# Output projection of a hybrid decoder layer by Strassen's seven products, with shared code and accumulating DMAs for the weight sums

## The chip, the core and the metric

The kernel runs on one NeuronCore of one Trainium2 chip. Five engines work from their own instruction queues and meet at semaphores: TensorE (PE: matmuls and transposes, results in PSUM banks of 128 x 512 float32), VectorE (DVE: elementwise work), ScalarE (ACT: activations, casts), GpSimd (POOL: here only reciprocal roots, and the issue of accumulating DMAs), SyncE (SP: the issue of plain DMAs). The metric is the device time of one execution in microseconds.

## The reference

One layer over 512 tokens and 1024 channels, in float32:

```python
u = _rmsnorm(h, norm1_g[l]);  proj = u @ w_in[l]           # GLU | q k v | r | decay | gates A, B
y_conv = silu(layernorm(dwconv31(glu))) @ w_conv_out[l]
y_gla  = (headwise_rmsnorm(gla(q, k, v, decay)) * silu(r)) @ w_gla_out[l]
merged = sigmoid(gate_a) * y_conv + sigmoid(gate_b) * y_gla
h = h + merged @ w_o[l]                                    # the output projection, 1024 x 1024
u2 = _rmsnorm(h, norm2_g[l])
z = dwconv3(u2 @ w_ffn_up[l])                              # 2 x 2816 channels
h = h + (silu(z[..., :F]) * z[..., F:]) @ w_ffn_down[l]    # the down projection, 2816 x 1024
return _rmsnorm(h, final_g)
```

## The kernel before

Every matrix product is done as three matmuls in the float32r type: each operand is split into a high part (an ACT cast, `whi` for weights) and a low part (a DVE subtraction, `wlo`), and `mm3` (L281 to 287) adds low x high, high x low and high x high into one PSUM bank. Activations lie with channels on partitions, 8 tiles of 128 channels by 512 tokens.

The weights form one long list, `order`. `load` issues the DMA of the next entry on SP into a `raw` tile (three buffers), `split_weight` splits it into `whi`/`wlo` (four buffers each), and `weight` hands the next entry to the products after it has split two entries ahead (`LOOK`). All queues run in order; in the loops spoken of here the framework's planner sets the order of the instructions on each engine from the data they share.

The stages around the change are: `w_gla` and `w_ga` products; eight `w_conv` column tiles of 24 matmuls (`col_tile`), each followed on DVE by a gate product, a sum and a split (`split`); the output projection; then the up projection with its 3-tap convolution and gate, in three `GROUPS` of channel pairs, each followed by a down projection.

The output projection before goes by `row_half`: for each half `n` of the output columns, four token tiles, eight channel tiles, three matmuls. In the second half the token tiles come one after another; `o_done` (L794) loads the residual `x`, adds it to the bank, squares it on ACT, and for `n == 1` forms the root on POOL (`rsqrt`, L333) and the normed tile `un` on DVE. `to_channels` (L355) transposes `un` on PE, four transposes to a bank, casts it on ACT (`uh`) and subtracts on DVE (`ul`). Tiles 0 and 1 are transposed inside the products of tiles 2 and 3, tile 2 at the end, and tile 3 after the second column tile of the up projection, whose first four column tiles (`w_up`, 256 tokens at a time) use tokens 0 to 255 first.

The down projection before (`down`, L902) already goes by Strassen's seven products in Winograd's form: the 512 tokens are two halves, the channels of a group two halves (the first and second of each pair), the output columns two halves. `STEPS` names the products `a11`, `a12`, `s1`, `n2`, `s4`, `n3`, `a22`, each with one or two weight blocks (`d`). `first_of_pair` and `second_of_pair` form the sums of activations. The weight sums are made in three ways: by accumulating DMAs on POOL (`kept` after `a11`, L226; `raw` of `n3`, L193), by a DVE addition at `n2` (L200) and by a DVE addition at `a22` (L200).

Of the kernel before, what the change touches and what calls it, by code (L numbers as in the profile page):

```python
# [10 lines left out]
F32 = mybir.dt.float32  # L11
# [20 lines left out]
EPS = 1e-6  # L32
GROUPS = (((0, 2), (1, 3), (4, 6), (5, 7)), ((8, 10), (9, 11), (20, 21)), ((12, 14), (13, 15), (16, 18), (17, 19)))
# [5 lines left out]
ET = mybir.EngineType  # L39

# [22 lines left out]
def trunk_layer(ctx: ExitStack, tc: tile.TileContext, a: dict, out: bass.AP):  # L63
# [84 lines left out]
    for m in range(KT):  # L148
        order += [("w_conv", m)]
    order += [("w_o", j) for j in range(KT)]  # L150
    for gi, pairs in enumerate(GROUPS):
        order += [("w_up", j) for pair in pairs for i in pair for j in (i, FT + i)]
        order += [("w_down", (gi, step, d)) for step, d in STEPS]
# [5 lines left out]
    def load():  # L159
        if len(raws) < len(order):  # L160
            name, j = order[len(raws)]
            if name == "w_down":
                raws.append(load_down(*j))
                return
            raw = wp.tile([P, D], F32, tag="raw", name=nm("raw"), bufs=3)
            nc.sync.dma_start(raw, a[name][j])
            raws.append(raw)


    def down_block(gi, d, row, col):  # L170

        pairs = GROUPS[gi][2 * d : 2 * d + 2]
        first = pairs[0][row]
        j = col * (FT // 2) + first // 2
        if len(pairs) == 2:
            return a["w_down"][j]
        return a["w_down"][j][:, row * T : (row + 1) * T]

    def load_down(gi, step, d):

        if step in ("s1", "s4"):
            return None
        row, col = {"a11": (0, 0), "a12": (1, 0), "n2": (1, 1), "n3": (0, 1), "a22": (1, 0)}[step]
        src = down_block(gi, d, row, col)
        if step in ("a11", "n2"):
            raw = fp.tile([P, D], F32, tag="kept", name=nm("kept"), bufs=4)
            kept[gi, d, "t" if step == "a11" else "b22"] = raw
        else:
            raw = wp.tile([P, D], F32, tag="raw", name=nm("raw"), bufs=3)
        n = src.shape[-1]  # L190
        nc.sync.dma_start(raw[:, :n], src)
        if step == "n3":
            nc.gpsimd.dma_start(raw[:, :n], down_block(gi, d, 1, 1), accum_op=ALU.add)  # L193
        return raw[:, :n]

    def sum_down(raw, gi, step, d):

        n = T * len(GROUPS[gi][2 * d : 2 * d + 2])
        t = kept[gi, d, "t"][:, :n]
        add = lambda o, x, y: nc.vector.tensor_tensor(o, x, y, ALU.add)  # L200
        if step == "s1":
            return t
        if step == "n2":
            add(t, t, raw)
            return t
        if step == "s4":
            return kept[gi, d, "b22"][:, :n]
        if step == "a22":
            add(raw, raw, t)
        return raw  # L210

    def split_weight(between=None):
        if len(ready) < len(order):
# [3 lines left out]
            if order[len(ready)][0] == "w_down":  # L217
                raw = sum_down(raw, *order[len(ready)][1])
# [5 lines left out]
                gi, step, d = order[len(ready)][1]  # L224
                if step == "a11":
                    nc.gpsimd.dma_start(raw, down_block(gi, d, 0, 1), accum_op=ALU.add)  # L226
# [521 lines left out]
    res_scope, rp = scoped("residual", 1, "right")  # L748
    ctx.push(res_scope)
# [19 lines left out]
    for m in range(KT):  # L769
# [4 lines left out]
        ma[m] = split(sg)  # L774
# [3 lines left out]
    u2 = new_acts()  # L778
    hres = {}
    ss2 = {}  # L780

# [11 lines left out]
    def o_done(t, n, acc):  # L793
        xr = tmp()  # L794
        nc.sync.dma_start(xr, a["x"][t * P : (t + 1) * P, n * T : (n + 1) * T])
        hres[t, n] = rp.tile([P, T], F32, tag="hres", name=nm("hres"), bufs=2 * NT)
# [284 lines left out]
```

## Time and profile before

The median of three runs is 852.83 us (851.73 to 852.95). The profiled execution took 851.61 us, with a span of 849.9 us from the first to the last instruction and a granted TensorE clock of 0.998.

| engine | busy us | share of the span | instructions |
|---|---|---|---|
| PE, matmuls | 838.7 | 99% | 3838 |
| PE, weight loads | 693.6 | 82% | 3838 |
| DVE | 630.3 | 74% | 881 |
| ACT | 374.2 | 44% | 517 |
| POOL | 29.6 | 3% | 48 |

On the page, a group's line gives the source line, engine, operation, output and inputs by name, shape and count, then its busy time, the mean of one in ns, and the idle time before it with what ended it. In a timeline a row has its start, its duration, engine, line, names and, in brackets, the idle time before it. A row can merge two instructions that follow on each other (x2). The duration of an instruction is longer than its start-to-start pitch, because instructions of one engine overlap.

### The profile page before, as it was taken

How to read it: one execution, taken by the hardware profiler on the slowest of the kernel's cores; microseconds unless marked ns; L12 is line 12 of the kernel's file. 1: busy time of each engine (PE TensorE's matmuls, PEld its weight loads, DVE VectorE, ACT ScalarE, POOL GpSimd, SP SyncE). 2: the span in 40 equal slices, each digit the busy share in tenths (PEclk: the TensorE clock that was granted, in tenths of full speed). 3: DMA queues.
4: the chain of work that ended last, by engine and by line, in shares of the span. 5: the costliest groups of instructions: out<-in, count | busy, mean ns of one | idle time of the engine just before them, and what ended most of it. 6: DMA issues, size and time to landing. Idle time of an engine off the chain costs nothing.

```text
span 849.9 us, 9915 instructions
## 1 busy us (share of the span) xinstructions
PE 838.7 (99%) x3838; PEld 693.6 (82%) x3838; DVE 630.3 (74%) x881; ACT 374.2 (44%) x517; POOL 29.6 (3%) x48
## 2 busy tenths in 40 slices
PE   8999999999999999999999999999999999999996
PEld 5888888888888888788888898888888888888885
DVE  5489879999998788734553458778857778677795
ACT  5522337435533522359322336444334443444454
POOL 1000000000100100000000000000000100000101
PEclk9999999999999999999999999999999999999999
DMA  7333232322222433322332263335542426422513
GB/s 273 102 106 101 97 99 86 100 74 99 76 76 77 134 99 99 99 75 79 120 124 94 68 223 124 100 103 120 171 132 95 109 65 237 138 89 96 124 49 124
DMA packets 27713, 94.63 MB, mean 111 GB/s; under 512 B 3137, under 2 KB 3265, under 8 KB 27666
## 3 DMA queue, kind: packets, MB, share of 16 engines
q1 hardware_dynamic: 25938, 88.23, 31.2%
q0 software_dynamic: 1728, 5.77, 4.0%
q8 instruction: 30, 0.49, 0.2%
q14 instruction: 17, 0.14, 0.0%
HBM read 91.89 MB, written 2.10 MB: 111 GB/s over the span
## 4 chain that ended last, share of the span: by engine, by line
PE 96%; DVE 1%; DMA 1%; ACT 1%; issue 0%; POOL 0%; POOLq 0%; SPq 0%; ACTq 0%; DVEq 0%
PE mm L285 30%; PE mm L287 30%; PE mm L286 30%; PE ax L691 1%; PE ax L362 1%; PE ax L673 1%; PE ax L693 1%; PE ax L287 1%; PE ax L286 1%; PE ax L285 1%; PE ax L660 0%; PE ax L708 0%; DMA x<-in_x_dram 0%; PE ax L659 0%; DMA raw<-in_w_v_dram 0%
## 5 line engine op out<-in xcount | busy, mean ns | idle before, releaser
L285 PE MATMUL mm<-uh,wlo 128*128 128x512 f32 (+1 forms) x768 | 294.8, 384 | 0.0
L287 PE MATMUL mm<-uh,whi 128*128 128x512 f32 (+1 forms) x768 | 292.4, 381 | 0.0
L286 PE MATMUL mm<-ul,whi 128*128 128x512 f32 (+1 forms) x768 | 292.0, 380 | 0.0
L240 ACT CAST whi<-raw 128x1024 fp32r<-128x1024 f32 x124 | 129.5, 1045 | 165.6 <-PE mm L287 132.7
L243 DVE TENSOR_TENSOR wlo<-raw,whi 128x1024 fp32r<-128x1024 f32 x124 | 151.1, 1220 | 52.2 <-ACT whi L240 51.7
L287 PEld LDWEIGHTS mm<-uh,whi 128*128 128x128 f32 x768 | 144.4, 188 | 28.1
L286 PEld LDWEIGHTS mm<-ul,whi 128*128 128x128 f32 x768 | 144.5, 188 | 27.3
L285 PEld LDWEIGHTS mm<-uh,wlo 128*128 128x128 f32 x768 | 144.5, 188 | 27.0
L450 DVE SCALAR_TENSOR_TENSOR c<-h,pp,c 128x511 f32<-128x511 f32 (+14 forms) x240 | 162.6, 733 | 0.7
L830 DVE SCALAR_TENSOR_TENSOR tmp<-mm,pp,tmp 128x511 f32<-128x511 f32 x88 | 65.8, 748 | 67.9 <-ACT tmp L828 66.7
L828 ACT ACTIVATE tmp<-mm,pp 128x512 f32<-128x512 f32 x44 | 34.2, 778 | 62.4 <-PE mm L287 62.4
L222 ACT CAST whi<-raw 128x1024 fp32r<-128x1024 f32 (+1 forms) x18 | 17.4, 978 | 28.5 <-PE mm L287 23.2
L333 POOL TENSOR_TENSOR rstd<-var,mhalf 128x1 f32<-128x1 f32 (+1 forms) x20 | 15.0, 758 | 377.7 <-DVE var L698 196.7
L223 DVE TENSOR_TENSOR wlo<-kept,whi 128x1024 fp32r<-128x1024 f32 (+1 forms) x24 | 26.7, 1130 | 0.0
L222 ACT CAST whi<-kept 128x1024 fp32r<-128x1024 f32 (+1 forms) x24 | 22.9, 973 | 8.6 <-DVE kept L200 7.9
L286 PE MATMUL mm<-wlo,sh 128*128 128x512 f32 x66 | 26.0, 394 | 0.0
L287 PE MATMUL mm<-whi,sh 128*128 128x512 f32 x66 | 26.0, 394 | 0.0
L924 DVE TENSOR_TENSOR hres<-hres,mm 128x512 f32<-128x512 f32 x36 | 24.3, 682 | 2.3 <-PE mm L287 2.1
L285 PE MATMUL mm<-whi,sl 128*128 128x512 f32 x66 | 25.9, 394 | 0.0
L285 PE MATMUL mm<-whi,ul 128*128 128x512 f32 x64 | 25.3, 395 | 0.5 <-DVE ul L367 0.5
L285 PE MATMUL mm<-h,wlo 128*128 128x512 f32 x64 | 25.7, 402 | 0.0
L285 PE MATMUL mm<-whi,h 128*128 128x512 f32 x64 | 25.4, 397 | 0.0
(200 smaller groups left out, 1113.5 us busy)
## 6 DMA issues: line engine op xcount, KB each, us to landing
raw<-in_w_up_dram SPq DMA_DIRECT2D x44, 512.0 KB, 3.4
raw<-in_w_glu_dram SPq DMA_DIRECT2D x16, 512.0 KB, 3.4
raw<-in_w_down_dram SPq DMA_DIRECT2D x15, 512.0 KB, 3.3
kept<-in_w_down_dram SPq DMA_DIRECT2D x10, 512.0 KB, 4.1
raw<-in_w_v_dram SPq DMA_DIRECT2D x8, 512.0 KB, 3.4
raw<-in_w_qk_dram SPq DMA_DIRECT2D x8, 512.0 KB, 3.3
raw<-in_w_r_dram SPq DMA_DIRECT2D x8, 512.0 KB, 3.4
raw<-in_w_gb_dram SPq DMA_DIRECT2D x8, 512.0 KB, 3.3
```

The source lines that it names most:

```text
L222: nc.scalar.copy(hi, raw)
L223: nc.vector.tensor_tensor(lo, raw, hi.bitcast(F32), ALU.subtract)
L240: nc.scalar.copy(hi, raw)
L243: pace[0] = nc.vector.tensor_tensor(lo, raw, hi.bitcast(F32), ALU.subtract)
L285: nc.tensor.matmul(acc, ll, rh, start=first, stop=False, **kw)
L286: nc.tensor.matmul(acc, lh, rl, start=False, stop=False, **kw)
L287: nc.tensor.matmul(acc, lh, rh, start=False, stop=last, **kw)
L333: nc.gpsimd.tensor_tensor(r, v, mhalf[:, :n], ALU.pow)
L450: nc.vector.scalar_tensor_tensor(y[:, s:], c[:, : T - s], w, y[:, s:], ALU.mult, ALU.add)
L828: nc.scalar.activation(z, acc, AF.Identity, bias=pp[:, PP_FB + m : PP_FB + m + 1], scale=w[2])
L830: nc.vector.scalar_tensor_tensor(z[:, s:], acc[:, : T - s], w[j], z[:, s:], ALU.mult, ALU.add)
L924: nc.vector.tensor_tensor(hn, hn, bank[of[step]][i], op)
```

## The change

1. `w_conv`'s column tiles are taken in the order of the pairs `O_PAIRS`, and for each pair the merged activations and their sums (`s1`, `n2`, `n3`, `s4`) are formed and split as soon as both tiles are there. The sums take the four `u` buffers that the first norm's activations had.
2. The output projection goes by the same seven products, with a function `seven` that the down projection shares. `hres` is loaded with `x` beforehand, in the residual pool, which now opens after the `late` pool has closed; all products are added to it.
3. The norm of tokens 0 and 1 is formed at `n3`; tile 0 is transposed after `a22`'s products on token tile 0, tile 1 after those on tile 1, tiles 2 and 3 inside the up projection's first four column tiles.
4. The weight sums: `a22`'s is made by an accumulating DMA on POOL, too, into the `kept` tile of `a11`, issued after `n2`'s split. `n2`'s stays on DVE. `kept` has two buffers instead of four, `raw` four instead of three; the block of `n2` and `s4` stays in its `raw` buffer.

```diff
+O_PAIRS = ((0, 2), (1, 3), (4, 6), (5, 7))
+SEVEN = {"w_o": KT // 2, "w_down": FT // 2}
...
-    order += [("w_o", j) for j in range(KT)]
+    order += [("w_conv", m) for pair in O_PAIRS for m in pair]
+    order += [("w_o", (O_PAIRS, step, d)) for step, d in STEPS]
...
+    def raw_tile():
+        return wp.tile([P, D], F32, tag="raw", name=nm("raw"), bufs=4)
...
+    def keep_tile(name):
+        if name == "w_o":
+            return tp.tile([P, D], F32, tag="x", name=nm("kept"), bufs=3)
+        return fp.tile([P, D], F32, tag="kept", name=nm("kept"), bufs=2)
+
+    LOADS = {"a11": (0, 0), "a12": (1, 0), "n2": (1, 1), "n3": (0, 1)}
+
+    def load_block(name, pairs, step, d):
+        if step not in LOADS:
             return None
+        src = block(name, pairs, d, *LOADS[step])
+        n = src.shape[-1]
+        if step == "a11":
+            dst = keep_tile(name)[:, :n]
+            kept[pairs, d] = dst
+        else:
+            dst = raw_tile()[:, :n]
+        nc.sync.dma_start(dst, src)
+        if step == "n3":
+            nc.gpsimd.dma_start(dst, block(name, pairs, d, 1, 1), accum_op=ALU.add)
+        if step == "n2":
+            kept[pairs, d, "b22"] = dst
+        return dst
+
+    def operand(raw, pairs, step, d):
+        if step == "s4":
+            return kept[pairs, d, "b22"]
+        if step == "n2":
+            nc.vector.tensor_tensor(kept[pairs, d], kept[pairs, d], raw, ALU.add)
+        return raw if step in ("a12", "n3") else kept[pairs, d]
+
+    def sum_on(name, pairs, step, d):
         if step in ("a11", "n2"):
+            nxt = block(name, pairs, d, *((0, 1) if step == "a11" else (1, 0)))
+            nc.gpsimd.dma_start(kept[pairs, d], nxt, accum_op=ALU.add)
...
-        if step == "a22":
-            add(raw, raw, t)
...
+    for p, q in O_PAIRS:
+        f1 = merged(p)
+        both = heap(F32R)
+        pair = {"a11": split_into(f1[:, :H], both[:, :H], both[:, H:])}
+        f2 = merged(q)
+        e1, e2 = tmp(), tmp()
+        s1, n2, n3, s4 = e1[:, :H], e1[:, H:], e2[:, :H], e2[:, H:]
+        nc.vector.tensor_tensor(s1, f1[:, H:], f2[:, H:], ALU.subtract)
+        nc.vector.tensor_tensor(n2, s1, f1[:, :H], ALU.subtract)
+        pair["a12"], pair["a22"] = halves(split(f2))
+        nc.vector.tensor_tensor(n3, f1[:, :H], f1[:, H:], ALU.subtract)
+        nc.vector.tensor_tensor(s4, f2[:, :H], n2, ALU.add)
+        u = up.tile([P, 4, T], F32R, tag="u", name=nm("sums"), bufs=4)
+        pair["s1"], pair["n2"] = halves(split_into(e1, u[:, 0, :], u[:, 1, :]))
+        pair["n3"], pair["s4"] = halves(split_into(e2, u[:, 2, :], u[:, 3, :]))
+        mixed.append(pair)
+    late_scope.close()
+    res_scope, rp = scoped("residual", 1, "right")
...
+    def seven(name, pairs, acts, complete, at=lambda step, i: None):
+        bank = {"x": [mm_bank(), mm_bank()], "y": [mm_bank(), mm_bank()], "z": [ax_bank(), ax_bank()]}
+        of = {"a11": "x", "n2": "x", "n3": "x", "a22": "x", "s1": "y", "s4": "y", "a12": "z"}
+        into = {
+            "a11": (0, 0, ALU.add, False),
+            "a12": (0, 0, ALU.add, True),
+            "s1": (1, 1, ALU.add, False),
+            "n2": (0, 1, ALU.subtract, False),
+            "s4": (0, 1, ALU.add, True),
+            "n3": (1, 1, ALU.subtract, True),
+            "a22": (1, 0, ALU.add, True),
+        }
...
+            for i in range(2):
+                products(step, i, parts)
+                if parts[-1][0] == 1:
+                    at(step, i)
+                    half, n, op, whole = into[step]
+                    t = 2 * half + i
+                    nc.vector.tensor_tensor(hres[t, n], hres[t, n], bank[of[step]][i], op)
+                    if whole:
+                        complete(t, n)
...
+    for t in range(NT):
+        for n in range(2):
+            hres[t, n] = rp.tile([P, T], F32, tag="hres", name=nm("hres"), bufs=2 * NT)
+            nc.sync.dma_start(hres[t, n], a["x"][t * P : (t + 1) * P, n * T : (n + 1) * T])
...
+    def o_complete(t, n):
         square_sum(("n2", t), hres[t, n], n)
+        if n == (0 if t > 1 else 1):
+            roots[t] = total_rstd(("n2", t))
+            if t > 1:
+                normed[t] = norm2(t, roots[t])
+
+    def o_at(step, i):
+        if (step, i) == ("n3", 0):
+            for t in range(2):
+                normed[t] = norm2(t, roots[t])
+        if (step, i) == ("a22", 0):
+            u2.extend(new_acts())
+            to_channels(normed[0], u2, 0)
+        if (step, i) == ("a22", 1):
+            to_channels(normed[1], u2, 1)
+
+    seven("w_o", O_PAIRS, mixed, o_complete, o_at)
...
-                    if lo == 0 and j == 1:
-                        to_channels(normed[NT - 1], u2, NT - 1)
+                    if lo == 0 and j > 1:
+                        to_channels(normed[j], u2, j)
```

188 lines of the change are left out of this document (62 added, 126 removed).

## The prediction

> **What bounds the kernel.** I read the page first (shares, then the chain of waits), then the table of stages, then the timelines of the engines where the output projection hands over to the up projection.
>
> ```profile
> span 849.9 us, 9915 instructions
> PE 838.7 (99%) x3838; PEld 693.6 (82%) x3838; DVE 630.3 (74%) x881; ACT 374.2 (44%) x517; POOL 29.6 (3%) x48
> PEclk9999999999999999999999999999999999999999
> PE 96%; DVE 1%; DMA 1%; ACT 1%; issue 0%; POOL 0%; POOLq 0%; SPq 0%; ACTq 0%; DVEq 0%
> ...
> 401.00:445.70 44.70, 44.70 (x195) 36.27 (x194) 24.92 (x31) 15.13 (x19) 0.00 (x0) 1.00 0.35 118
> 445.70:493.00 47.30, 47.30 (x217) 38.55 (x216) 22.20 (x30) 16.08 (x28) 1.66 (x3) 1.00 0.25 80
> 586.00:624.50 38.50, 38.50 (x167) 31.26 (x166) 32.58 (x38) 15.86 (x16) 0.00 (x0) 1.00 0.54 160
> ```
>
> PE (TensorE) is the chain: 96% of it, at full clock. The last three lines are stretches (window, then its length, then busy time of PE, weight load, DVE (VectorE), ACT, POOL): the `w_conv` products, the output projection, and a down projection that already goes by seven products. PE is busy in every microsecond of all three. So a matmul that goes is worth its pitch, and a wait that comes is worth its length; DVE work is free until PE waits for it. DVE has 22.20 of 47.30 us in the output projection now.
>
> **What the change removes.** One matmul's pitch comes from two DVE rows that both start when a `w_conv` column tile of 24 matmuls ends:
>
> ```profile
> 440.37 0.69 DVE L772 TENSOR_TENSOR h<-mm,h 128x512 f32<-128x512 f32 x1 [2.39 <-PE mm L287]
> 445.92 0.69 DVE L772 TENSOR_TENSOR h<-mm,h 128x512 f32<-128x512 f32 x1 [2.39 <-PE mm L287]
> ...
> L286 PE MATMUL mm<-wlo,sh 128*128 128x512 f32 x66 | 26.0, 394 | 0.0
> L286 PE MATMUL mm<-wlo,h 128*128 128x512 f32 x64 | 25.2, 394 | 0.0
> ```
>
> (445.92 - 440.37)/24 = 0.231 us. The two groups below have the same mean, 394 ns, in the seven products (`sh`) and in the output projection (`h`), so the pitch holds for the new products. Before, the projection has 4 token tiles x 2 column halves x 8 channel tiles x 3 = 192 matmuls. After: 7 products x 2 token tiles x 4 channel tiles x 3 = 168. Gone: 24 x 0.231 = 5.55 us. The 32 transposes of the hand-over stay.
>
> **What it adds on DVE.** Start-to-start in the hand-over of before:
>
> ```profile
> 485.83 0.69 DVE L797 TENSOR_TENSOR hres<-mm,tmp 128x512 f32<-128x512 f32 x1 [1.31 <-PE mm L287]
> 487.37 0.16 DVE L790 SCALAR_TENSOR_TENSOR var<-ss 128x1 f32<-128x1 f32 x1 [0.85 <-ACT junk L785]
> 488.26 1.41 DVE L804 SCALAR_TENSOR_TENSOR un<-hres,rstd,gain 128x512 f32<-128x512 f32 x2 [0.73 <-POOL rstd L333]
> 489.59 2.35 DVE L243 TENSOR_TENSOR wlo<-raw,whi 128x1024 fp32r<-128x1024 f32 x2
> ...
> 492.09 1.16 PE L362 MATMUL ax<-ident,un 128*128 128x128 f32 x8
> 493.01 0.36 PE L285 MATMUL mm<-uh,wlo 128*128 128x256 f32 x1
> 493.33 0.28 PE L287 MATMUL mm<-uh,whi 128*128 128x256 f32 x1
> 493.45 0.28 PE L285 MATMUL mm<-uh,wlo 128*128 128x256 f32 x1
> ...
> 493.06 0.68 DVE L797 TENSOR_TENSOR hres<-mm,tmp 128x512 f32<-128x512 f32 x1
> 493.66 1.22 DVE L243 TENSOR_TENSOR wlo<-raw,whi 128x1024 fp32r<-128x1024 f32 x1
> 494.79 0.68 DVE L367 TENSOR_TENSOR ul<-ax,uh 128x512 fp32r<-128x512 f32 x1
> 495.39 0.15 DVE L790 SCALAR_TENSOR_TENSOR var<-ss 128x1 f32<-128x1 f32 x1
> ...
> L864 DVE TENSOR_TENSOR v<-v,w 128x256 f32<-128x256 f32 x11 | 4.7, 424 | 0.2
> ```
>
> So: a 512-wide sum 0.60, a 1024-wide one 1.13 (489.59 to 491.86 is two of them), one half of `un` 0.67, `var` 0.10, a 256-wide one under 0.42; a residual sum to `var` 1.54 (its square on ACT lies between), `var` to `un` 0.89 (the root on POOL). PE: 0.92 for 8 transposes, 0.12 for a 256-wide matmul.
>
> In the `w_conv` stage a pair of channel tiles now takes two weight splits, four sums and three splits 512 wide, and five sums 256 wide: 2x1.13 + 7x0.60 + 5x0.42 = 8.6 us beside 48 matmuls of 11.1 us. Hidden. In the projection itself, from its first matmul to the middle of its last product (`a22`), DVE's queue in the built program holds 15 sums 1024 wide, 17 of 512, 4 of 256 and 4 halves of `un`: 17.0 + 10.2 + 1.7 + 2.7 = 31.6 us, beside 156 matmuls of 36.0 us. It still fits, but DVE is at 88% where it was at 47%, and whatever is late goes on to the end. Three places follow, each with what DVE must do and what PE has meanwhile:
>
> - *First token tile of `a22`.* Its matmuls accumulate on the bank that `n3` filled, so the DVE sum reading that bank must be done. The sum is queued behind the norm of tokens 0 and 1, and behind two weight splits. From the end of `s4` on tile 0: residual sum to `var` 1.54, to `un` 0.89, two halves 1.33, residual sum 0.60, split 1.13, `var` 0.10, split 1.13, two halves 1.33, then the sum itself, 0.69: 8.74. PE has 36 matmuls and a transpose, 8.4, less 0.16 since a result is ready 0.39 after the start and not 0.23. PE waits 0.5.
> - *Start of the up projection.* Its first half needs tokens 0 to 255, and tile 1 is transposed only after `a22` ends (before, tile 2 came last and was not needed yet). On DVE, from the end of `a22` on tile 0: residual sum to `var` and to `un` 2.43 (and some 0.2 more, since ACT now copies a transposed group in between), half `un` 0.67, `ul` of tile 0 0.60, half `un` 0.67, residual sum 0.60, third weight split 1.13, then `ul` of tile 1, 0.69: 7.0. PE has 7 + 8 transposes and 4 of tile 2 that were put ahead here, 2.1, 12 matmuls 2.8, and 3 small matmuls 0.35: 5.2. PE waits 1.8 to 1.9.
> - *Second half of the up projection's first four tiles.* Tile 3 is now transposed right before it; before, two column tiles later was time enough:
>
> ```profile
> 498.85 1.03 PE L362 MATMUL ax<-ident,un 128*128 128x128 f32 x8
> 499.48 0.59 ACT L366 CAST uh<-ax 128x512 fp32r<-128x512 f32 x1 [3.98 <-PE ax L362]
> 500.10 0.69 DVE L367 TENSOR_TENSOR ul<-ax,uh 128x512 fp32r<-128x512 f32 x1 [1.26 <-ACT uh L366]
> ```
>
> From the transposes to a usable `ul`: 500.10 + 0.69 - 498.85 = 1.94. PE has the transposes, 0.92 less its first pipe, and four matmuls that need `uh` only: 1.3. PE waits 0.6.
>
> Sum of waits: 0.5 + 1.9 + 0.6 = 3.0.
>
> **Loads and queues.** DMA issues (count, size, median us from issue to landing), the two accumulating lines (ns), and the start of the first down group:
>
> ```profile
> raw<-in_w_down_dram SPq DMA_DIRECT2D x15, 512.0 KB, 3.3
> ...
> raw<-in_w_down_dram POOLq DMA_DIRECT2D x5, 512.0 KB, 5.3
> kept<-in_w_down_dram POOLq DMA_DIRECT2D x5, 512.0 KB, 5.5
> ...
> tmp<-in_x_dram SPq DMA_DIRECT2D x8, 256.0 KB, 3.4
> ...
> raw<-in_w_down_dram SPq DMA_DIRECT2D x3, 256.0 KB, 2.6
> ...
> L193 POOL DMA_DIRECT2D raw<-in_w_down_dram x6: 854/876/1058, 568.4 to 805.4; - x6
> L226 POOL DMA_DIRECT2D kept<-in_w_down_dram x6: 844/850/861, 570.8 to 796.3; - x6
> ...
> 582.31 0.40 PE L285 MATMUL mm<-whi,yl 128*128 128x512 f32 x1
> 584.41 0.88 POOL L193 DMA_DIRECT2D raw<-in_w_down_dram  x1 [8.17 <-DVE tmp L830]
> ```
>
> `x` now goes straight into `hres`: eight loads at once, and since the residual pool opens in the `late` pool's place they can start only when `w_conv`'s last matmul ends. Behind them on SP stands the second `n3` load. The first lands 3.4 us later, each further one 0.7 more (512 KB against 256 KB of `w_down`: 3.3 and 2.6), and the gain vector, 512 KB, goes ahead of them: the third, which tile 1 needs, at 3.4 + 1.4 + 1.4 = 6.2. DVE comes to it after two 1024-wide, six 512-wide and four 256-wide instructions: 2.3 + 3.6 + 1.7 = 7.6. Cost 0, with 1.4 us of cover; a late load delays DVE, which has 36.0 - 31.6 = 4.4 us to spare in the stage.
>
> The sum for `a22` moves from DVE to POOL's queue: six sums of 1.22 at most leave the down stages, where PE does not wait (38.50 of 38.50): 0. In exchange `b22` stays in a `raw` buffer, and the second `n3` load waits on SP for the second `a12` split; its accumulating DMA then stands on POOL behind the first `n2` sum, which waits for DVE. By the queues' orders it starts some 13.5 us after a group's first product and not 2 (584.41 against 582.31). It lands 5.4 later, and with POOL's issue of 0.9 at 18.9 to 19.8; its split can start when `n2`'s buffers come free, after 96 matmuls, 22.2. Cover 2.4 in the three down groups; in the projection it starts earlier, 4.4. `a22`'s own sums start at 17.3 and land at 22.7, wanted after 120 matmuls, 27.7. POOL's roots stand behind these issues, but all of them are issued before the first root is due. Cost 0, open upward (below). At the kernel's end the last sum, square and scale keep their order: 0.
>
> Sum: -5.55 + 3.0 = -2.5 us. On the profiled execution, 851.61 us with 849.9 of span (the 1.7 around it stays), that is 849.1. That execution is 1.2 under the median of the three runs, 852.83, so the forecast for the median is 850.3.
>
> **Rivals.**
> - *The waits do not come* (the order on DVE is kinder than its queue reads): the whole 5.55 is kept, 847.3. For it: before, the hand-over shows no PE wait at all. Against: DVE stands in order, and the third weight split lies ahead of tile 1's `ul`.
> - *No change:* the `x` loads land late and push DVE. If the third comes 7 us after DVE asks for it, 4.4 go into the slack and 2.6 onto the waits, 5.6 in all: 852.9. For it: SP issues eight loads in one burst at the moment when they are needed. Against: 80 GB/s in that stage before.
> - *Slower:* the second `n3` sum lands late in the down stages. It decides once load and accumulation take 2.4 us more than the rows say; each microsecond beyond that is paid in each of three groups. Twice the accumulating DMA's time (5.4 more) gives 3 x (5.4 - 2.4) + 1.0 in the projection = 10, from 850.3: 860. For it: the sum starts 11 us later than before, and 12 accumulating DMAs (twice x6) become 24. Against: a landing within 5.3 to 5.5 in the median.
> - *The clock drops while PE waits.*
>
> ```profile
> 0.00:4.00 4.00, 1.45 (x2) 0.83 (x3) 0.17 (x1) 1.28 (x1) 1.35 (x9) 1.00 0.44 137
> ```
>
> Here PE is busy 1.45 of 4.00 us and the granted clock stays 1.00. If the waits at the up projection did cut it to half over the first 24 small matmuls, 24 x 0.12 = 2.9 us would be added: 853.2. The Trainium skill, TensorE: Matmul & The Clock Gate, section HAM oscillation, says that a PE idle for more than about 3.4 us goes back to half rate. By that rule the waits here, all under 2 us, change nothing. The trace agrees: every slice of the clock line above shows 9.
>
> **Chances and range.** Waits as summed, within a microsecond and a half: 0.64. Whole gain: 0.08. No change: 0.15, of which 0.04 beyond the bound. Slower by the late sums: 0.10. Clock: 0.03 (no change). A change of 0.2% (1.7 us) is about what a measurement here can tell, the three runs spanning 1.2. Faster 0.64 + 0.08 = 0.72, same 0.14, slower 0.14. The range runs from the whole gain, 847.6 with its edge cut, to no change, 852.6; what lies outside is the slow case, half of the no-change case and part of the whole gain.
>
> **What will show it.** Right: 24 matmuls fewer; the window from the projection's first matmul to the up projection about 3 us shorter, not 5.5; PE idle some 2 us before the first up products, released by DVE `ul` and the weight split, 0.5 before `a22`, 0.6 at tile 3; DVE near 88% in the projection; down stages without PE idle. Wrong: PE idle before `n3` in a down group released by ACT or a DMA; DVE waiting on `x` loads by more than 4 us; a row with a clock under 1.00; or the hand-over without idle.

## The result, and the profile after

The changed kernel takes 850.03 us in the median of six runs (848.98 to 850.37), the kernel before 853.17 us in six runs beside it (851.73 to 853.59): a ratio of 0.9964, 95% interval 0.9954 to 0.9974. The forecast was 850.3, faster. The profiled execution took 850.15 us with a span of 848.4, so it is 1.46 us faster than the profiled one of before (851.61); the forecast for that pair was 2.5. The table at the end of this section and the first experiments say why the pair and the medians differ.

The page of the changed kernel (busy time and share; the clock line; the chain of waits), and three stretches (window, length, busy time of PE, weight load, DVE, ACT, POOL, clock, DMA share, GB/s): `w_conv`, the output projection up to the first up product, the first down projection.

```profile
span 848.4 us, 9947 instructions
PE 835.3 (98%) x3814; PEld 691.0 (81%) x3814; DVE 646.1 (76%) x913; ACT 383.3 (45%) x531; POOL 42.6 (5%) x60
PEclk9999999999999999999999999999999999999999
PE 96%; DVE 1%; DMA 1%; ACT 1%; issue 0%; POOL 0%; SPq 0%; POOLq 0%; ACTq 0%
```

```profile
402.48:447.18 44.70, 44.70 (x196) 36.24 (x194) 31.96 (x49) 17.95 (x25) 1.91 (x2) 1.00 0.38 110
447.18:489.80 42.62, 41.13 (x189) 33.55 (x188) 36.40 (x50) 23.46 (x36) 6.00 (x7) 1.00 0.68 197
581.65:620.68 39.03, 39.03 (x169) 31.65 (x168) 30.20 (x37) 16.53 (x17) 3.47 (x4) 1.00 0.63 175
```

There are 3838 - 3814 = 24 matmuls fewer. `w_conv` takes 44.70 us as before, though DVE has 31.96 us of work there and not 24.92: that part is hidden. The projection's stretch is 4.68 us shorter (42.62 against 47.30) with 5.55 us of matmuls gone; PE is idle for 1.5 us of it, and DVE, 47% busy before, is at 85%. The prediction's sign for this stretch was about 3 us shorter. It got shorter than that since only 0.31 us of the second forecast wait lies ahead of the first up product, the rest between the first up products, and since 4 transposes fewer lie in it (20 instead of 24). The down projection, with `a22`'s sum moved to a DMA, has no PE idle.

The timeline of PE in the changed kernel where the projection hands over (start, duration, names, idle time before it and what ended it):

```profile
480.15 0.27 PE L369 MATMUL ax<-ident,un 128*128 128x128 f32 x1
481.59 0.48 PE L292 MATMUL mm<-whi,h 128*128 128x512 f32 x1 [1.18 <-DVE hres L859]
...
488.02 1.47 PE L369 MATMUL ax<-ident,un 128*128 128x128 f32 x12
489.80 0.50 PE L292 MATMUL mm<-uh,wlo 128*128 128x256 f32 x2 [0.31 <-ACT uh L373]
490.92 0.39 PE L292 MATMUL mm<-uh,wlo 128*128 128x256 f32 x1 [0.62 <-DVE wlo L250]
491.52 0.39 PE L293 MATMUL mm<-ul,whi 128*128 128x256 f32 x1 [0.22 <-DVE ul L374]
...
503.21 1.03 PE L369 MATMUL ax<-ident,un 128*128 128x128 f32 x8
504.48 0.75 PE L292 MATMUL mm<-uh,wlo 128*128 128x256 f32 x4 [0.24 <-ACT uh L373]
505.20 0.39 PE L293 MATMUL mm<-ul,whi 128*128 128x256 f32 x1
```

All three forecast waits are there, each released by what was named: before `a22` by the sum that reads `n3`'s bank; at the start of the up projection by ACT's `uh`, the third split and `ul`; at tile 3 by `uh`, with a second gap of 0.24 ahead of the first `ul` product. The brackets count from the modelled end of the row before. Start to start, with 0.115 us a transpose and 0.12 a small matmul, the second place costs (489.80 - 488.02 - 1.38) + (490.92 - 489.80 - 0.24) + (491.52 - 490.92 - 0.12) = 1.8 us, the third (504.48 - 503.21 - 0.92) + (505.20 - 504.48 - 0.48) = 0.6. Both are as forecast. The first is 1.2 and not 0.5.

For all kernels of this study, the table gives the start of the projection's first product, and from there the distance to the first down product, to the start of the last matmul, and to the span's end (us):

| kernel | first product at | to first down product | to last matmul | to the end |
|---|---|---|---|---|
| before | 445.72 | 136.59 | 396.23 | 404.2 |
| after | 447.18 | 134.47 | 393.92 | 401.3 |
| before_early4 | 446.97 | 136.58 | 396.25 | 404.2 |
| before_warm | 447.87 | 136.58 | 396.25 | 404.2 |
| before_drop24 | 447.77 | 131.71 | 391.39 | 399.3 |
| after_raw3 | 447.64 | 134.46 | 393.90 | 401.6 |
| after_warm | 446.15 | 134.49 | 393.93 | 401.3 |
| after_third | 448.10 | 133.46 | 392.90 | 400.8 |
| after_hand | 448.71 | 132.74 | 392.18 | 399.5 |
| after_norm_t3 | 446.28 | 132.74 | 392.19 | 399.5 |
| after_best | 446.11 | 131.14 | 390.59 | 397.9 |
| after_sum_dve | 446.80 | 134.47 | 394.11 | 401.5 |
| after_twice | 446.69 | 134.46 | 405.78 | 413.5 |
| after_thrice | 446.92 | 134.48 | 421.98 | 429.3 |

Two things stand out. From the projection's first product on, equal code takes equal time within 0.03 us up to the last matmul, so these columns resolve what the medians can't. And before it, where nearly all the code is the same, the start wanders by 3 us. The pair of profiles has a change of -2.9 in the part that was changed, and +1.46 ahead of it.

### The profile page after: what moved, and what is told of

It reads as the page before. It is cut to its first block, busy times and chain, and to the rows that moved or that the text cites. A ratio compares the mean times of both kernels' runs of the same rounds, so it can differ in the third digit from the quotient of the medians.

```text
span 848.4 us, 9947 instructions
## 1 busy us (share of the span) xinstructions
PE 835.3 (98%) x3814; PEld 691.0 (81%) x3814; DVE 646.1 (76%) x913; ACT 383.3 (45%) x531; POOL 42.6 (5%) x60
## 4 chain that ended last, share of the span: by engine, by line
PE 96%; DVE 1%; DMA 1%; ACT 1%; issue 0%; POOL 0%; SPq 0%; POOLq 0%; ACTq 0%
PE mm L292 30%; PE mm L293 29%; PE mm L294 29%; PE ax L293 1%; PE ax L294 1%; PE ax L292 1%; PE ax L698 1%; DMA raw<-in_w_v_dram 1%; PE ax L680 1%; PE ax L700 1%; DVE hres L859 0%; PE ax L369 0%; PE ax L667 0%; PE ax L715 0%; PE ax L666 0%
## 5 line engine op out<-in xcount | busy, mean ns | idle before, releaser
L247 ACT CAST whi<-raw 128x1024 fp32r<-128x1024 f32 x116 | 120.8, 1045 | 134.6 <-PE mm L294 101.3
L250 DVE TENSOR_TENSOR wlo<-raw,whi 128x1024 fp32r<-128x1024 f32 x116 | 141.0, 1219 | 38.3 <-ACT whi L247 37.8
L231 ACT CAST whi<-kept 128x1024 fp32r<-128x1024 f32 (+1 forms) x32 | 31.6, 992 | 24.4 <-DVE kept L211 12.8
L232 DVE TENSOR_TENSOR wlo<-kept,whi 128x1024 fp32r<-128x1024 f32 (+1 forms) x32 | 36.6, 1152 | 2.8 <-ACT whi L231 2.8
L859 DVE TENSOR_TENSOR hres<-hres,mm 128x512 f32<-128x512 f32 x48 | 32.6, 682 | 5.6 <-PE mm L294 3.8
L231 ACT CAST whi<-raw 128x1024 fp32r<-128x1024 f32 (+1 forms) x24 | 23.6, 992 | 19.8 <-PE mm L294 19.5
L340 POOL TENSOR_TENSOR rstd<-var,mhalf 128x1 f32<-128x1 f32 (+1 forms) x20 | 17.6, 884 | 262.2 <-DVE var L705 195.6
L232 DVE TENSOR_TENSOR wlo<-raw,whi 128x1024 fp32r<-128x1024 f32 (+1 forms) x24 | 27.3, 1152 | 3.5 <-ACT whi L231 3.5
```

The lines of the kernel that those rows point to most:

```text
L231: nc.scalar.copy(hi, raw)
L232: nc.vector.tensor_tensor(lo, raw, hi.bitcast(F32), ALU.subtract)
L247: nc.scalar.copy(hi, raw)
L250: pace[0] = nc.vector.tensor_tensor(lo, raw, hi.bitcast(F32), ALU.subtract)
L340: nc.gpsimd.tensor_tensor(r, v, mhalf[:, :n], ALU.pow)
L859: nc.vector.tensor_tensor(hres[t, n], hres[t, n], bank[of[step]][i], op)
```

## Experiments on the first 447 us

The 1.46 us arise in the first 22 us of the kernel: from the transposes of the third token tile on, at 20.46 us before and 21.92 after, the two traces run alike up to the projection. The one thing that the change alters there is `raw`'s fourth buffer: the fourth weight load starts at 3 us and not at 9.

**The early fourth load alone, in the kernel before (before_early4).**

```diff
+            if len(raws) == 3:
+                raw = bp.tile([P, D], F32, tag="fourth", name=nm("raw"), bufs=1)
+            else:
                 raw = wp.tile([P, D], F32, tag="raw", name=nm("raw"), bufs=3)
```

> The kernel before, with one difference: the fourth weight load of the whole kernel goes into a buffer of its own, so it starts at 3 us with the first three and not at 9 us, as it does in the changed kernel with its four raw buffers. Nothing else of the change is in it. In the two traces the output projection begins at 445.72 before and 447.18 after, 1.46 us later, and all of it arises in the first 16 us. Theory A (the fourth load takes bandwidth from the three that the first products wait for): about 1.5 us slower than before, and the second whi cast on ACT waits for its raw load by over 1 us as it does after. Theory B (chance: the first products run at 0.43 us a matmul or at 0.23 depending on when in the execution PE got its full rate, whatever the loads do): no difference in the medians, and executions of either kernel fall into two groups some 1.5 us apart.

Measured: 852.65 us against 852.98, ratio 1.0001 (0.9993 to 1.001). No difference: theory A falls. The 18 executions of the kernel before in this measurement fall into two groups, as theory B has it: six at 851.46 to 851.73 us and twelve at 852.44 to 853.64.

**The changed kernel without it (after_raw3).**

```diff
-        raw = wp.tile([P, D], F32, tag="raw", name=nm("raw"), bufs=4)
+        raw = wp.tile([P, D], F32, tag="raw", name=nm("raw"), bufs=3)
...
+        elif step == "n2" and d == 0:
+            dst = qp[0].tile([P, D], F32, tag="b22", name=nm("b22"), bufs=1)[:, :n]
```

> The changed kernel with three raw buffers and one more for the first n2 block, that is opened only after the heads; so the loads of the first 16 us stand as in the kernel before, and everything else of the change is kept. Theory A (the early fourth load costs the 1.46 us at the start): about 1.5 us faster than the changed kernel, 848.5, and the output projection begins near 445.7. Theory B (chance): the same as the changed kernel, 850.0, with the start of the projection anywhere between 445.7 and 447.2.

Measured: 850.19 us (848.93 to 851.87), the same as the changed kernel's 850.03; the projection starts at 447.64. Theory A falls here, too.

**PE kept busy while it waits (after_warm).**

```diff
     to_channels(xs[0], u1, 0, (1,))
+    for _ in range(6):
+        nc.tensor.matmul(warm[:, :P], ident, ident, start=True, stop=True)
```

> The changed kernel with six more 128 x 128 matmuls whose result nobody reads, on PE between the transposes of the first token tile and the first product, where PE waits 1.27 us for ul in the changed kernel's trace. If the slow pitch of the first products (0.43 us a matmul from 10.63 to 15.06, ten of them, though the granted clock of that window reads 1.00) hangs on PE having been idle there: the full rate comes about 3 us earlier, 1.0 to 1.7 us faster, 848.3 to 849.0. If the late loads alone set the start: 0 to 0.3 us slower, 850.0 to 850.3.

Measured: 849.13 us (848.62 to 849.68), just above the 848.3 to 849.0 of the first theory. That is 0.9 under the changed kernel's 850.03, but the two were not measured beside each other and their ranges overlap, so the medians alone don't show the gain. Its first products go at 0.23 us. PE's first products in the changed kernel, the stretch of the slow ones, and the first of the kernel before:

```profile
10.63 0.79 PE L292 MATMUL mm<-whi,ul 128*128 128x512 f32 x1 [1.27 <-DVE ul L374]
...
12.08 0.63 PE L292 MATMUL mm<-whi,ul 128*128 128x512 f32 x1
12.50 0.63 PE L293 MATMUL mm<-wlo,uh 128*128 128x512 f32 x1
```

```profile
10.60:15.06 4.46, 4.43 (x10) 3.47 (x11) 3.79 (x6) 2.67 (x4) 0.55 (x1) 1.00 0.95 346
```

```profile
10.13 0.50 PE L285 MATMUL mm<-whi,ul 128*128 128x512 f32 x1 [0.55 <-DVE ul L367]
10.46 0.39 PE L286 MATMUL mm<-wlo,uh 128*128 128x512 f32 x1
```

12.50 - 12.08 = 0.42 us a matmul is half rate, and the granted clock of the stretch reads 1.00: that row does not show it. Of the eleven profiles without the six matmuls nine begin at half rate, whichever kernel it is (before_early4, after_raw3 and before_drop24 among them), two at full rate (before and after_norm_t3); of the three profiles with them, none begins at half rate. The Trainium skill, TensorE: Matmul & The Clock Gate, section What's actually happening, has PE at half rate until it has been busy through a window of some 3.4 us that runs freely, so that the number of slow matmuls differs from run to run. The rows agree that it differs: in the changed kernel products run from 10.63 without a break and the full rate comes at 15.06, 4.4 us later; over the nine profiles it comes 2.7 (after_twice) to 4.9 us (after_thrice) after the first product.

**The same in the kernel before (before_warm).** The edit is that of after_warm.

> The kernel before with the same six extra matmuls at the start that the run after_warm gave the changed kernel, so that both begin with the full rate and the chance of the first 16 us is out of the comparison. The change itself, read from the projection's first product on, was worth 404.2 - 401.2 = 3.0 us in the traces. Theory B (the start is chance and no part of the change): 851.5 to 852.3, that is 2.4 to 3.2 above the changed kernel with the same matmuls (849.1), and executions within 1 us of each other instead of 2. If the extra matmuls help only the changed kernel's start: 853 as before.

Measured: 853.00 us (852.01 to 853.80) against 853.07, ratio 1.0000. The expectation failed, though this kernel's first products do go at 0.23 us. What holds it is another wait: PE stands 1.25 us before the transposes of the third token tile, at 22.26. ACT's square of the third token tile, in before, after_raw3 and before_warm, which all have three buffers at the start:

```profile
16.85 1.06 ACT L400 ACTIVATE junk<-x 128x1024 bf16<-128x1024 f32 x1 [1.50 <-DMA x<-in_x_dram]
```

```profile
19.18 1.06 ACT L409 ACTIVATE junk<-x 128x1024 bf16<-128x1024 f32 x1 [2.33 <-DMA x<-in_x_dram]
```

```profile
19.46 1.06 ACT L400 ACTIVATE junk<-x 128x1024 bf16<-128x1024 f32 x1 [3.75 <-DMA x<-in_x_dram]
```

With three buffers the load of that tile stands on SP behind weight loads that wait for a buffer, and in three of four such profiles its square comes at 19.2 to 19.5; only in the profile of before it came at 16.85, and the projection then began 1.9 to 2.2 us earlier than in the other three. Its second `whi` cast, too, waited only 0.23 us for its load; in the other thirteen profiles, with three buffers or four, it waited 0.79 to 1.72. So the profile of before that the prediction stood on was a lucky execution, and nothing here puts any of the 1.46 us down to the change. With the same buffers at the start the change is worth 852.98 - 850.19 = 2.8 us (three in both: before and after_raw3, measured together) and 852.65 - 850.03 = 2.6 (four in both: before_early4 and after, measured apart). The table bears out that PE's rate at the start counts with four buffers: the three such kernels that begin at full rate reach the projection at 446.11 to 446.28, five that begin at half rate at 446.69 to 447.18 (after_third and after_hand lost 1.4 us elsewhere, see the last section). With three buffers and the late tile it makes no difference: 447.64 and 447.77 at half rate, 447.87 at full; the last rests on one profile.

## Experiments on the projection and its waits

Three of the kernels here, after_third, after_hand and after_norm_t3, were timed once (850.65, 849.94 and 847.52 us). They are read from the projection's first product on, where equal code repeats within 0.03 us.

**The 24 matmuls alone (before_drop24).** The kernel before without the last channel tile of the projection:

```diff
+            skip = 1 if name == "w_o" else 0
+            if k == nk - skip:
+                return
```

> The kernel before with the last of the eight channel tiles left out of the output projection: 24 matmuls fewer, and so another output; loads, splits, waits for x and the norms stay. This prices the 24 matmuls that the change removes by themselves. The prediction's price: 24 x 0.231 = 5.55 us, 847.6 against 853.2, with no new wait of PE in the hand-over. If DVE already set the pace there (rival), less: 849 to 851, with PE idle behind DVE.

Measured: 848.34 us; from the first product to the first down product 131.71 against 136.59, that is 4.88 us. Against the expectation, PE waits in its hand-over, where it never did before:

```profile
489.78 0.66 PE L365 MATMUL ax<-ident,un 128*128 128x128 f32 x4 [0.61 <-DVE ul L370]
```

4.88 + 0.61 = 5.5: the price of the matmuls is right, and a shorter projection uncovers DVE even with the old order.

**The third and fourth splits moved behind tile 1 (after_third).**

```diff
-            ws = [weight("w_up", j, 0) for i in pairs[0] for j in (i, FT + i)]
+            ws = [weight("w_up", j, 0) for j in ups[:2]]
...
+                    if len(ws) == j:
+                        with tc.issue_after(tile1[0].ins), tc.issue_after(tile1[1].ins):
+                            ws.append(weight("w_up", ups[j], 0))
```

> The changed kernel with the third and fourth w_up splits put behind tile 1's uh and ul on ACT and DVE, where the third stood ahead of them. Read from the trace: the PE waits at the start of the up projection, 0.31 + 0.62 + 0.22 = 1.15 us in the changed kernel. Theory 1 (the prediction's: the third split ahead of tile 1's ul makes this wait): one split's 1.13 us goes, and 0 to 0.2 is left. Theory 2 (tile 1 is transposed right before it is needed, and transposes, cast and subtraction take 1.94 us with little work for PE beside them): 0.7 to 0.9 us is left. The first wait (1.18 before a22) and the one at tile 3 (0.24 + 0.24) stay by both.

**Tile 1 transposed earlier (after_hand).**

```diff
             to_channels(normed[0], u2, 0)
-        if (step, i) == ("a22", 1):
             to_channels(normed[1], u2, 1)
```

> The changed kernel with tile 1 transposed together with tile 0, after a22's products on token tile 0, so that 24 matmuls lie between its transposes and the up projection; the third w_up split keeps its place on ACT and DVE behind the last residual sum. Read from the trace: the PE waits at the start of the up projection, 1.15 us in the changed kernel. Theory 2 (place of the transposes): 0 to 0.2 us is left, the projection ends 1 us earlier. Theory 3 (DVE is behind as a whole, whatever its order, and PE waits for it somewhere): 0.8 us or more is left, in this place or in front of it. The wait of 1.18 before a22 stays by both.

The waits of PE that are left between the projection's start and the end of the first four up tiles, of after_third and then of after_hand (the place of tile 3, 0.24 in both, is left out):

```profile
482.51 0.47 PE L292 MATMUL mm<-whi,h 128*128 128x512 f32 x1 [1.17 <-DVE hres L860]
491.30 0.39 PE L293 MATMUL mm<-ul,whi 128*128 128x256 f32 x1 [0.38 <-DVE ul L375]
```

```profile
483.12 0.47 PE L292 MATMUL mm<-whi,h 128*128 128x512 f32 x1 [1.17 <-DVE hres L859]
```

Without the split, 0.38 of 1.15 is left (1.01 us gained to the first down product): between the two theories and nearer to theory 1; both have a share, by the brackets 0.77 for the split and 0.38 for the place. With the transposes moved nothing is left (1.73 gained), since tile 1's `ul` then comes ahead of the split as well. So theory 3 falls in this place, and the earlier transposes are the cheaper cure: the split stays where it was.

**The norm of tile 1 behind the sum, tile 3 earlier (after_norm_t3).**

```diff
-            for t in range(2):
-                normed[t] = norm2(t, roots[t])
+            normed[0] = norm2(0, roots[0])
+        if (step, i) == ("n3", 1):
+            normed[1] = norm2(1, roots[1])
...
-                    if lo == 0 and j > 1:
-                        to_channels(normed[j], u2, j)
+                    if lo == 0 and j == 2:
+                        to_channels(normed[2], u2, 2)
+                        to_channels(normed[3], u2, 3)
```

> The changed kernel with two moves: the norm of token tile 1 (two halves of un, 1.33 us) comes on DVE after the sum that reads n3's bank on tile 0, not before; and tile 3 is transposed together with tile 2, one column tile earlier. Read from the trace: the wait before a22 (1.18 us in the changed kernel, 0.5 predicted) and the waits at tile 3 (0.24 + 0.24). By the prediction's queue both go. The sum now also no longer stands behind a root on POOL, which took 1.41 us beside a DVE split where roots beside nothing took 0.57. Theory 3 (DVE is behind as a whole): of the 1.18 us some 0.3 to 0.8 come back at the start of the up projection, which grows from 1.15 to 1.5 to 1.9. If DVE has time in hand: 1.15 stays 1.15.

The first and third waits are gone. The second grew from 1.15 to 0.21 + 1.02 + 0.22 = 1.45: a quarter of the first came back, as theory 3 has it, since DVE does the same work. Gained to the first down product: 1.73.

Why was the first wait 1.18 and not 0.5? DVE and, in the second fence, POOL in the changed kernel, from `s4`'s sum on tile 0 to `n3`'s:

```profile
472.18 0.69 DVE L859 TENSOR_TENSOR hres<-hres,mm 128x512 f32<-128x512 f32 x1
473.72 0.16 DVE L880 SCALAR_TENSOR_TENSOR var<-ss 128x1 f32<-128x1 f32 x1 [0.85 <-ACT junk L875]
...
477.70 0.15 DVE L880 SCALAR_TENSOR_TENSOR var<-ss 128x1 f32<-128x1 f32 x1
477.77 1.21 DVE L232 TENSOR_TENSOR wlo<-kept,whi 128x1024 fp32r<-128x1024 f32 x1
...
480.77 0.68 DVE L859 TENSOR_TENSOR hres<-hres,mm 128x512 f32<-128x512 f32 x1
```

```profile
474.03 0.57 POOL L340 TENSOR_TENSOR rstd<-var,mhalf 128x1 f32<-128x1 f32 x1 [9.67 <-DVE var L880]
478.00 1.41 POOL L340 TENSOR_TENSOR rstd<-var,mhalf 128x1 f32<-128x1 f32 x1 [3.40 <-DVE var L880]
```

480.77 + 0.68 - 472.18 = 9.27 us, where the prediction's queue gave 8.74. The order is as it had it. What it missed is the second root: started behind `var`, beside the split at 477.77, it lasts 1.41 us against 0.57 with nothing beside it, up to 0.43 us past the end of the split (479.41 against 478.98), and `un` behind it comes 0.5 late. The prediction let that root run under the split at no cost. No run takes the split away from that root, but other rows bear it out. After, a later root beside a split is as long; before, one beside the subtraction `ul`, which reads `ax` in a PSUM bank, is not:

```profile
492.30 1.37 POOL L340 TENSOR_TENSOR rstd<-var,mhalf 128x1 f32<-128x1 f32 x1 [5.21 <-DVE var L880]
```

```profile
495.71 0.55 POOL L333 TENSOR_TENSOR rstd<-var,mhalf 128x1 f32<-128x1 f32 x1 [7.49 <-DVE var L790]
```

**All moves together (after_best).** The edits of after_hand, after_norm_t3 and after_warm.

> The changed kernel with the moves together: tile 1 transposed with tile 0 after a22's products on tile 0; the norm of tile 1 behind n3's sum on tile 0; tile 3 transposed with tile 2; and the six extra matmuls at the start. All 24 matmuls saved, and if the three waits (1.18, 1.15, 0.48) go with these moves the part from the projection's first product to the end is 398.5 to 398.9 us, against 401.2 in the changed kernel and 404.2 before; the time 846.4 to 847.0, against 849.1 with the extra matmuls alone. Theory 3 (DVE is behind as a whole): 0.8 us or more of the waits stays, 847.5 or more.

Measured: 845.87 us (845.75 to 847.18) against 853.68 of the kernel before, measured beside it, ratio 0.9905 (0.9886 to 0.9924). Faster than both kernels, and than expected. Its projection (as above, to the first up product):

```profile
446.11:486.55 40.44, 40.44 (x186) 33.16 (x184) 34.92 (x48) 22.76 (x35) 6.00 (x7) 1.00 0.72 206
```

To the first down product it takes 131.14, 5.45 less than before of the 5.55 that the matmuls are worth. What the change gave back was nearly all order, not work.

## Experiments on the weight sums

**`a22`'s sum on DVE again, in the down projections (after_sum_dve).**

```diff
-        if step in ("a11", "n2"):
+        if step == "a11" or (step == "n2" and name == "w_o"):
...
+        if raw is not None and step == "a22":
+            nc.vector.tensor_tensor(raw, raw, kept[pairs, d], ALU.add)
+            return raw
```

> The changed kernel with a22's weight sum of the three down projections made on DVE again, as before the change: the block is loaded once more on SP and added on DVE (six sums 1024 or 512 wide, at most 1.22 us each), and six accumulating DMAs leave POOL's queue. The prediction's step: this move was worth 0, PE does not wait in these stages. So the lengths of the down stages stay 39.03, 29.27 and 38.81 us, and DVE is some 6 us busier over the kernel. If the move to the DMA helped or hurt, they change by up to 1.2 us each.

Measured, in one execution (850.04 us), from the first down product of a group to the next up product, in the last group to the last matmul: 39.03, 29.46 and 38.81 us. Only the second group, of three channel pairs, differs, by 0.2 (29.27; before: 29.47). The move was worth 0.2 us, not 0; where they come from is not shown.

**The second `n3` sum made late (after_twice, after_thrice).**

```diff
-            nc.gpsimd.dma_start(dst, block(name, pairs, d, 1, 1), accum_op=ALU.add)
+            for _ in range(2 if name == "w_down" and d == 1 else 1):
+                nc.gpsimd.dma_start(dst, block(name, pairs, d, 1, 1), accum_op=ALU.add)
```

> The changed kernel with the accumulating DMA of the second n3 block done twice in each of the three down projections, the second one after the first has landed, so the sum is there one accumulating DMA (5.1 to 5.4 us) later; n3's weights then hold that block twice, and the output is another. The prediction's slower rival: cover 2.4, so 3 x (5.4 - 2.4) = 9 us slower. Read from the trace of the changed kernel instead: in the first down group the sum lands near 600.5, its split starts at 604.16 and PE needs it after 609.4 + 2.8, so some 9 us of cover down to PE: 0 us in the lengths of the three down stages (39.03, 29.27, 38.81).

> The same, with that accumulating DMA done three times, so the sum is there 10.2 to 10.8 us later; the output is another. By the prediction's cover of 2.4: 3 x 8 = 24 us slower. By a cover of 9 us down to PE: 1 to 2 us in each down stage, 3 to 6 us in all, with PE idle released by the split of n3's second block. If it is 0, not even three of them reach PE.

Measured, in one execution each (861.88 and 877.95 us): the three stages take 43.45, 34.23 and 41.29 us with two (4.42 + 4.96 + 2.48 = 11.9 more) and 49.14, 39.96 and 46.01 with three (28.0 more). My own reading ahead of the runs, 0 and 3 to 6, was wrong; the prediction's rule, 9 and 24, came near, in part by luck, as the rows show. The timeline of the first group of after_twice (rows of POOL, ACT and PE), and two stretches of it:

```profile
594.77 1.01 POOL L202 DMA_DIRECT2D raw<-in_w_down_dram  x1
...
602.32 0.85 POOL L202 DMA_DIRECT2D raw<-in_w_down_dram  x1 [2.52 <-DMA raw<-in_w_down_dram]
...
610.20 0.39 PE L295 MATMUL mm<-whi,yh 128*128 128x512 f32 x1
...
611.05 1.04 ACT L232 CAST whi<-raw 128x1024 fp32r<-128x1024 f32 x1 [7.70 <-DMA raw<-in_w_down_dram]
...
612.15 0.50 PE L293 MATMUL mm<-whi,yl 128*128 128x512 f32 x1 [1.57 <-ACT whi L232]
...
613.41 0.50 PE L294 MATMUL mm<-wlo,yh 128*128 128x512 f32 x1 [0.76 <-DVE wlo L233]
```

```profile
612.15:614.44 2.29, 1.52 (x5) 1.05 (x6) 2.29 (x3) 1.84 (x2) 0.00 (x0) 1.00 0.03 9
614.44:617.40 2.96, 2.96 (x9) 2.29 (x8) 2.96 (x4) 0.00 (x0) 0.00 (x0) 0.51 0.86 252
```

The accumulating DMA took 602.32 - 594.77 = 7.6 us, the second one 8.7, not the 5.4 of a median: right behind another accumulating DMA, and with the loads. In the changed kernel, where it is issued at 595.27, that lands it near 602.8, 1.3 us ahead of its split at 604.16, not 2.4; but the split isn't what PE waits for. With the split at 611.05 PE lost 1.95 - 0.23 + 1.26 - 0.23 = 2.75 us, the first 1.72 of it behind `whi` and 1.03 behind `wlo`, so a split begun by 611.05 - 2.75 = 608.3 would have cost nothing: down to PE the cover is some 5.5 us, an estimate from these rows. The other 1.7 us of the 4.42 are the clock: behind these two waits PE ran at half rate, 0.51 granted, for some 3 us. In the second group half rate (0.50 granted from 717 to 719) followed one wait of 2.62 us, in the third a wait of 2.24 us was followed by full rate (1.00 granted from 847 to 852.5):

```profile
714.98 0.49 PE L293 MATMUL mm<-whi,yl 128*128 128x512 f32 x1 [2.62 <-ACT whi L232]
...
847.05 0.47 PE L293 MATMUL mm<-whi,al 128*128 128x512 f32 x1 [2.24 <-DVE var L881]
```

## Why the prediction was right, step by step

- *The matmuls, -5.55:* right. 24 fewer; before_drop24 prices them at 4.88 and a wait of 0.61.
- *First token tile of `a22`, 0.5:* wrong by 0.7. The queue was read rightly, but a root on POOL beside a DVE split was priced at nothing; it cost 0.5 us of delay. The other 0.2 lies in the small terms of the sum and was not traced further.
- *Start of the up projection, 1.8 to 1.9; tile 3, 0.6:* right in size, 1.8 and 0.6 start to start, and each goes when its transposes move.
- *Sum of waits, 3.0:* 5.55 - (136.59 - 134.47) = 3.4, if the matmuls are worth 5.55; added up one by one, 1.2 + 1.8 + 0.6 = 3.6.
- *`x` loads, 0:* right, with the landing mis-sized: the loads took 7.6 us in the median, the third was to land after 6.2 and landed 8.7 us after the first was issued (447.37 to 456.04), and DVE waited once in the changed kernel, 1.22 us. That cost nothing: in after_raw3 DVE didn't wait for `x` at all and in after_warm 0.18 us, and PE's wait before `a22` is 1.17 and 1.18 all the same. The late load went into DVE's slack in the stage, so the no-change rival did not come. DVE's wait in the timeline, and the loads in the list of all DMA issues (count, size, median us to landing):

```profile
456.04 0.69 DVE L859 TENSOR_TENSOR hres<-hres,mm 128x512 f32<-128x512 f32 x1 [1.22 <-DMA hres<-in_x_dram]
```

```profile
hres<-in_x_dram SPq DMA_DIRECT2D x8, 256.0 KB, 7.6
```

- *`a22`'s sum to the DMA, 0:* 0.2 in the second group.
- *The late sum as slower rival, 10:* it did not occur. Made to occur, it cost 11.9 in the down stages where the rule gave 9; the cover of 2.4 was two errors, a landing put too early and a need put too early, which work against each other, and part of the price was the clock.
- *The kernel's end, 0:* wrong by 0.6. From the last matmul to the span's end it takes 7.96 us before and 7.34 after (7.3 to 7.9 in the other kernels of the new code). 0.5 of it is order on DVE: its last sum starts 0.97 us behind the start of the last matmul before (842.92 against 841.95) and 0.48 after (841.58 against 841.10). Before, tile 2's sum stood behind a product that waited 1.84 us for ACT; after, it waits for PE alone. The rest comes and goes with the last store. DVE's rows before, and after:

```profile
839.50 0.69 DVE L883 TENSOR_TENSOR hres<-hres,gain 128x512 f32<-128x512 f32 x1 [1.84 <-ACT junk L785]
840.11 0.68 DVE L924 TENSOR_TENSOR hres<-hres,mm 128x512 f32<-128x512 f32 x1
...
842.92 0.68 DVE L924 TENSOR_TENSOR hres<-hres,mm 128x512 f32<-128x512 f32 x1
```

```profile
838.75 0.69 DVE L859 TENSOR_TENSOR hres<-hres,mm 128x512 f32<-128x512 f32 x1 [0.56 <-PE mm L294]
...
841.58 0.68 DVE L859 TENSOR_TENSOR hres<-hres,mm 128x512 f32<-128x512 f32 x1
```

- *The clock, no change:* right for this kernel, where waits of 1.18 us and less left the up products at 0.12 us. The reason given was too strong. By the rule that the prediction cited (the Trainium skill, TensorE: Matmul & The Clock Gate, section HAM oscillation) idle times beyond some 3.4 us bring half rate; in after_twice two waits of 1.72 and 1.03 us close to each other did, and in the next group a single one of 2.62. The measurement decides: waits of less can do it. In the third group one of 2.24 us did not, though it is longer than either of the first two, so the longest wait alone doesn't settle it; what does is open.

Sum: -5.55 + 3.4 - 0.2 - 0.6 = -2.9 from the projection's first product on, where -2.5 was forecast: the waits cost 0.4 more, and two terms put at 0 gave 0.8. For the profiled pair 849.1 was forecast and 850.15 came, because the start of the profile of before was a lucky one; for the median, to which 1.2 had been added because that execution lay so much under it, 850.3 was forecast and 850.03 came. That this is so close is in part luck: the medians lie 853.17 - 850.03 = 3.1 us apart and not 2.5, and the kernel before came out at 853.17 in six runs and not at 852.83.

## What to carry to other kernels

Saving matmuls on a PE-bound stretch uncovers the next engine in the hand-over: price the new order of that engine instruction by instruction, and then look for the transposes or sums that can move one product ahead, since 3.3 of the 3.4 us given back here was order (after_best). Compare two traces from the first instruction that the change touches, not from the kernel's start: here the first 29 us differ by 2 us between executions of equal code. And follow a late transfer to the engine that bounds the stage, not to the first buffer that it could hold up.

## What the runs showed of the hardware

- Half rate at the start is not in the granted clock (1.00 in the profile, 0.42 us a matmul); half rate behind later waits is (0.51 and 0.50 in after_twice).
- A root on POOL was slower beside a weight split on DVE: 1.37 and 1.41 us, against 0.55 to 0.57. In after_third, and likewise in after_hand, two roots took 4.87 us that take 1.84 in the changed kernel (196.87) with the same instructions around them, and PE waited 0.98 us for what hangs on them, far ahead of anything that these two kernels change; their projection starts 1.4 us later by it. Rows of after_third:

```profile
196.35 4.87 POOL L340 TENSOR_TENSOR rstd<-var,mhalf 128x2 f32<-128x2 f32 x2 [114.00 <-DVE var L706]
201.78 1.13 PE L716 MATMUL ax<-ident,o 128*128 128x128 f32 x6 [0.98 <-ACT o L710]
```

The Trainium skill, GPSIMD Engine Reference, section Specifications, says that GpSimd shares its SBUF interfaces with VectorE and contends with DVE instructions that read two SBUF inputs. The split at 477.77, with `kept` and `whi` as inputs, is one, and the root beside it agrees, as does the one beside `ul`, with one input in PSUM; why the same stretch at 196 us is sometimes 3 us longer stays open.

- The accumulating DMAs of L201 in the changed kernel, of 512 and 256 KB, land 5.2 us after their issue in the median, but up to 8.0; those behind one another in after_twice took 7.6 and 8.7.

```profile
DMA to landing us min/median/max: 3.6/5.2/8.0
```
